# Gate rows of a fused transformer layer moved from the FFN loop to the output projection, and operand-making in wider operations

## The chip, the cores and the metric

The kernel runs on one core of a Trainium2 chip. The metric is device microseconds (us) of one execution. The kernel before took 2268.96 us, the median of three runs between 2266.91 and 2269.43.

Each engine runs its own queue in order: TensorE (PE, with its weight loads as PEld) multiplies, VectorE (DVE) and ScalarE (ACT) work on elements, SyncE (SP) issues the transfers, GpSimd (POOL) does next to nothing here. They wait for each other through semaphores.

## The reference

One layer on x of 512 positions x 2048 features, with a conditioning vector c:

```python
mod = cond @ w_ada[layer] + b_ada[layer]          # cond = silu(c); 6 x 2048 values
sh1, sc1, g1, sh2, sc2, g2 = split(mod, 6)
h = rms_norm(x, norm1_g) * (1 + sc1) + sh1
proj = h @ w_in                                   # 2048 -> 4*1024 + 3*1024
o_hg = hgrn2_mixer(...)                           # 8 heads, gated recurrence
o_sb = stick_breaking_mixer(...)                  # 8 heads, causal attention
x = x + g1 * (concat(o_hg, o_sb) @ w_out)
h = rms_norm(x, norm2_g) * (1 + sc2) + sh2
gate, up = split(h @ w_ffn_in, 2)                 # 2048 -> 2 * 5632
x = x + g2 * ((silu(gate) * up) @ w_ffn_out)
```

What matters here is `mod`: six groups of 2048 values, each a dot product of c with a column of `w_ada`. G1 is needed for the first residual, SC2 and SH2 for the second norm, and G2 only at the very end.

## The kernel before

All matrix products are of fp32 accuracy: each operand is split in a high and a low part (`S.copy` to fp32r on ACT, then `V.tensor_sub` on DVE), and three matmuls (hi x hi, hi x lo, lo x hi) stand for one. A weight split is line 231 (ACT) and line 232 (DVE); `three` and `product` issue the matmuls, all recorded under line 93.

A **row** of `mod` is one call of `ada(comp, k)` (line 186): 128 of the values, from a 1 MiB load into a buffer of the "raw" ring (four buffers, shared with all weight loads; line 175) and a multiply-and-sum on DVE over 128x2048 elements (line 179, called a gemv here). There are 16 rows to each of the six groups, 96 in all. `rest` is the list of those not yet done.

The program goes through these stages, with times of the profiled execution:

1. Norm, first projections and stick-breaking heads, up to about 440 us.
2. **Gated stage**, 440 to 770 us: eight HGRN2 heads. `hg_project` gives PE long runs of projection matmuls with 512 columns; `hg_attend` is a chain of "levels" (five small steps of DVE, ACT and PE that wait for each other), put between the projection matmuls. Where each step goes is fixed as the program is built: `Clock` adds up a modelled time of the matmuls, and a side task that yields a number from the table `Y` continues when the clock has passed it. `tasks_every(Y["hgtask"], rest[:HG_TASKS])` is such a side task: one row every 30 units, 8 of them (SC2 rows 8 to 15).
3. **Output projection**, 770 to 952 us: 16 column tiles m, each of 16 k-blocks (48 matmuls of 512 columns, about 10.9 us). A tile loads its weight (`wo8r` is tile 8's), splits it in two halves a tile ahead, and ends with the residual on DVE (line 874), a store of x1 to DRAM, a square on ACT and a sum on DVE. The loop over m then takes rows from `rest`: before, two behind m = 0 and 1 and one behind m = 2 to 13, the 16 SH2 rows.
4. **Second norm and first two FFN tiles**, 946 to 1001 us. The last column tile is done in two halves of 256 positions. `normed` multiplies a 128x256 block by the norm (DVE) and applies gain and shift (ACT, line 899); `make_first` and `make_second` split the blocks into the operands that `first_part` multiplies by `wff`. The results are held until DVE has formed the operands for products 6, 7, 5 and 4 (opB, opC).
5. **FFN loop**, 1001 to 1827.6 us: matrices f = 2 to 43. Each loads 2 x 1 MiB (`wg`, `wu`), forms sums of weight blocks, splits seven of them, and multiplies in seven products of 24 matmuls with 256 columns, in the order 1, 2, 6, 7, 5, 4, 3 (Strassen's scheme). Products 1, 6, 5, 3 add up in one accumulator, ffA, and ACT copies its value out between them (`tap`, line 1030: a, b, u); ffB has product 2, ffC 7 and 4 (tap c). `keep` multiplies the activations of a pair of matrices, and `one_later` spreads what follows of it (names `forms`, `fhi`) over the next matrix. Behind each matrix one row of `rest` is taken: before, the 16 G2 rows behind f = 2 to 17.
6. FFN output, 1827 to 2266 us.

Within a stage a scheduler sets the order of each engine's queue by priority and by the program's order; the ring's buffers set when a load can be issued.

Of the kernel before, what the change touches and what calls it, by code (L numbers as in the profile page):

```python
# [24 lines left out]
HT = 256  # L25
HALF = 8
# [1 line left out]
ORDER = (2, 1, 7, 6, 4, 5, 3)  # L28
AHEAD = 300
SC2_EARLY = 8  # L30
HG_TASKS = 8
EARLY = 3
Y = {"norm": 7.0, "qk": 5.0, "z": 4.0, "aA": 10.0, "oA": 2.0, "aB": 4.5, "oB": 2.5,
     "base": 6.5, "level": 2.2, "r1": 3.0, "r2": 2.4, "ho": 1.8,
     "settle": 20.0, "shrow": 6.0, "fix": 2.6, "hgtask": 30.0, "task": 5.0}
EPS = 1e-6
TINY = 1e-30
LN_TINY_CAP = 44.0
# [7 lines left out]
SH1, SC1, G1, SH2, SC2, G2 = range(6)  # L46
# [35 lines left out]
def view(t, off, dims):  # L82
    return bass.AP(tensor=t.tensor, offset=t.offset + off, ap=[list(t.ap[0])] + [list(d) for d in dims])
# [46 lines left out]
def trunk(ctx, tc, a):  # L130
    nc = tc.nc
    V, S, G = nc.vector, nc.scalar, nc.gpsimd
# [31 lines left out]
    gain2 = const.tile([P, KT], F32, name="gain2")  # L164
# [132 lines left out]
    for k in range(KT):  # L297
        xk = xo[:, k]
        if k == 0:
# [3 lines left out]
            j = SC1 * KT  # L303
# [196 lines left out]
    rb = sb.tile([P, T], F32, tag="I", name="rb1", bufs=1)  # L500
# [28 lines left out]
    shrow = xo[:, 0:4].rearrange("p a b -> p (a b)")  # L529
# [256 lines left out]
    hgx = ExitStack()  # L786
    hg = hgx.enter_context(tc.tile_pool(name="hg", bufs=1))
    clock.start(hg_heads())
    rest = [partial(ada, SC2, k) for k in range(SC2_EARLY, KT)] + [partial(ada, SH2, k) for k in range(KT)]
    clock.start(tasks_every(Y["hgtask"], rest[:HG_TASKS]))  # L790
    for h in range(NH):
        if h:
# [49 lines left out]
    x1 = xop.tile([P, KT, T], F32, tag="xo", name="x1")  # L842
# [23 lines left out]
    for m in range(KT - 1):  # L866
        xr = load_x(m)
        if m < 2:
            wo_part(m, 0, [last])
        else:  # L870
            if m > 3:
                wo_part(m, 8, head)
            wo_part(m, 0, tail)
        V.scalar_tensor_tensor(x1[:, m], wo[m], mcol(G1, m), xr, op0=ALU.mult, op1=ALU.add)
        nc.sync.dma_start(x1d[:, m], x1[:, m])
        add_square(m)
        for _ in range(2 if m < 14 and len(rest) > 14 - m else 1):
            if rest:
                rest.pop(0)()

# [8 lines left out]
    def block(kh, th, j):
        return x1[:, kh * HALF + j, th * HT:th * HT + HT]  # L890

    def split_to(p, j, src):
        S.copy(H[p][:, j, 0], src)
        V.tensor_sub(H[p][:, j, 1], src, H[p][:, j, 0].bitcast(F32))

    def normed(kh, th, j):
        k, hs = kh * HALF + j, slice(th * HT, th * HT + HT)
        V.tensor_mul(x1[:, k, hs], x1[:, k, hs], rb[:, hs])
        S.activation(x1[:, k, hs], x1[:, k, hs], AF.Identity, scale=gain2[:, k:k + 1], bias=mcol(SH2, k))

    def make_first(j):
        for kh in range(2):
            normed(kh, 0, j)
            split_to(1 + kh, j, block(kh, 0, j))
            parts[kh, 0, j] = H[1 + kh][:, j, 0], H[1 + kh][:, j, 1]

    def make_second(j):
        normed(0, 1, j)
        t = ft.tile([P, 2, HT], F32R, tag="t", name=f"b12_{j}")
        S.copy(t[:, 0], block(0, 1, j))  # L910
        V.tensor_sub(t[:, 1], block(0, 1, j), t[:, 0].bitcast(F32))
        parts[0, 1, j] = t[:, 0], t[:, 1]
        normed(1, 1, j)
        split_to(3, j, block(1, 1, j))
        parts[1, 1, j] = H[3][:, j, 0], H[3][:, j, 1]
# [10 lines left out]
    m = KT - 1  # L926
# [4 lines left out]
    rb = ft.tile([P, T], F32, tag="ss2", name="rb2", bufs=2)  # L931
    for i, hs in enumerate(halves):
        out = acc(f"wo{m}h{i}")[:, 0:HT]
        n = 0
        for c0, (whi, wlo) in ((8, w8), (0, w0)):
            for kk in range(8):
                three(out, whi[:, kk], wlo[:, kk], ohi[:, c0 + kk, hs], olo[:, c0 + kk, hs], n == 0, n == KT - 1)
                n += 1
        V.scalar_tensor_tensor(x1[:, m, hs], out, mcol(G1, m), xr[:, hs], op0=ALU.mult, op1=ALU.add)
        nc.sync.dma_start(x1d[:, m, hs], x1[:, m, hs])  # L940
        sq = ft.tile([P, HT], F32, tag="t", name=f"sql{i}")
        S.activation(sq, x1[:, m, hs], AF.Square)
        ps = att(f"ssum2{i}")[:, 0:HT]
        PE.matmul(ps, ones, ss2[:, hs], start=True, stop=False)
        PE.matmul(ps, ones, sq, start=False, stop=True)
        av = ft.tile([P, HT], F32, tag="t", name=f"av2{i}")
        tmp = ft.tile([P, HT], F32, tag="t", name=f"tmp2{i}")
        y = rb[:, hs]
        S.activation(y, ps, AF.Ln, bias=epsb, scale=1.0 / D)
        V.tensor_scalar(av, ps, 1.0 / D, EPS, op0=ALU.mult, op1=ALU.add)  # L950
        S.activation(y, y, AF.Exp, scale=-0.5)
        newton(y, av, tmp)
        if i == 0:
            for k in range(EARLY):
                make_first(k)

    for j in range(HALF):
        if j >= EARLY:
            make_first(j)
        make_second(j)  # L960


    first = [[acc(f"ff{j}")[:, 0:HT] for j in range(4)], [att(f"ff{j + 4}")[:, 0:HT] for j in range(2)]]
# [32 lines left out]
    for j in range(HALF):
        V.tensor_sub(block(0, 0, j), block(0, 1, j), block(0, 0, j))
        t2 = ft.tile([P, HT], F32, tag="t", name=f"t2_{j}")
        V.tensor_sub(t2, block(1, 1, j), block(0, 0, j))
        split_to(6, j, t2)  # L1000
        V.tensor_sub(block(1, 0, j), block(1, 0, j), t2)
    for j in range(HALF):
        V.tensor_sub(block(0, 1, j), block(1, 1, j), block(0, 1, j))
        split_to(7, j, block(0, 1, j))
    for j in range(HALF):
        split_to(5, j, block(0, 0, j))
    for j in range(HALF):
        split_to(4, j, block(1, 0, j))
# [47 lines left out]
    def begin_second():  # L1056
# [11 lines left out]
        for q in range(4, 7):  # L1068
            load_op(0, q)
        yraw.append(fg.tile([P, 2, 4, T], F32, tag="b22", name="yraw"))  # L1070

    rest += [partial(ada, G2, k) for k in range(KT)]

    forms = {}

# [53 lines left out]
    for f in range(2, FM):  # L1131
        A11, A12 = halves_of(load(a["w_fi"][f, 0], [P, KT, P], f"wg{f}"))
        A21, A22 = halves_of(load(a["w_fi"][f, 1], [P, KT, P], f"wu{f}"))
        S1 = tp.tile([P, HALF, P], F32, tag="sum", name=f"ffS{f}", bufs=3)
        A, B, C = acc(f"ffA{f}")[:, 0:HT], acc(f"ffB{f}")[:, 0:HT], att(f"ffC{f}")[:, 0:HT]
        w1, w2 = operand(A11, f"ff{f}_1"), operand(A12, f"ff{f}_2")
        with tc.high_priority(offset=AHEAD):
            V.tensor_add(S1, A21, A22)
# [12 lines left out]
        t_c = tap(C, f"c{f}")
        one_later()
        product(A, operand(S1, f"ff{f}_5"), 5)
        tu = tap(A, f"u{f}")
        one_later()
        product(C, operand(A22, f"ff{f}_4"), 4)
        one_later()
        product(A, operand(A12, f"ff{f}_3", False), 3)

        sg = tp.tile([P, T], F32, tag="sg", name=f"sg{f}", bufs=2)  # L1160
        up = tp.tile([P, T], F32, tag="up", name=f"up{f}", bufs=1)
        with tc.high_priority(offset=2 * AHEAD if f == FM - 1 else 0):
            V.tensor_add(sg[:, 0:HT], B, ta)
            S.activation(sg[:, 0:HT], sg[:, 0:HT], AF.Silu)
# [82 lines left out]
    for u, (c, i) in enumerate(units):  # L1247
# [16 lines left out]
        t2 = (T2[0] if u else yraw[0][:, 2])[:, 0:CHUNKS[c]]  # L1264
# [113 lines left out]
```

## Time and profile before

| | |
|---|---|
| median of three runs | 2268.96 us |
| profiled execution | 2268.31 us |
| its span in the trace | 2266.5 us |
| mean granted TensorE clock | 0.994 |
| DMA, mean over the span | 193 GB/s, 437.68 MB |
| rows of `mod` by line 179 | 95, 217 us of DVE (mean 2286 ns) |
| DVE waiting for a row's load | 36 us |

The span runs from the first to the last instruction that the profiler recorded; the execution's own time is 1.8 us longer. Busy times are shares of the span. A wait is told as "engine, line it waits at <- engine and line that released it: total, times, longest". In a timeline row stand the start, the duration, the engine, the line, and what is read and written; brackets at its end give the wait just before it and what ended it. A window row gives busy time (and number of instructions) of each engine in a stretch, the granted clock of PE, the DMA engines' busy share and their rate. SPq is the queue of transfers that SP issues.

### The profile page before, as it was taken

Reading aid. Unit: us, or ns where it says so; the run is one execution under the profiler, and the core shown is the slowest. Engines: PE = TensorE matmul, PEld = TensorE weight load, DVE = VectorE, ACT = ScalarE, POOL = GpSimd, SP = SyncE. Lnnn points to the kernel's source line nnn. Section 1 sums busy time; section 2 is a strip of 40 time slices with the busy share of each in tenths; the row PEclk is TensorE's granted clock in tenths of the full one; section 3 lists DMA queues with packets and bytes.
Section 4 is the critical chain, followed back from the end, with each engine's and each line's share of the span. In section 5 each row is a group of like instructions: output and inputs, shape, how many; then the busy total and the mean of one; then the engine's idle time right before and its main releaser. Section 6 shows DMA issues by size and latency. Waiting matters only on the chain. (4 is left out here: it accounts for less than half of the span.)

```text
span 2266.5 us, 35532 instructions
## 1 busy us (share of the span) xinstructions
PE 2221.9 (98%) x14171; PEld 2025.4 (89%) x14171; DVE 1912.1 (84%) x2566; ACT 1157.3 (51%) x2015; POOL 10.1 (0%) x25
## 2 busy tenths in 40 slices
PE   7999899999999999999999999999999999999999
PEld 6899899978888888899999999999999987788887
DVE  8886778899888875599899988888888888898888
ACT  4315666566565622475444545555455554545453
POOL 0000000000000000000000000000000000000000
PEclk9999999999999999999999999999999999999999
DMA  9885546763232296326565554535454486666452
GB/s 371 314 319 215 178 142 232 288 228 112 93 112 75 83 327 250 111 103 228 205 215 201 195 181 145 176 131 177 142 172 150 159 333 248 241 223 223 163 198 67
DMA packets 115265, 437.68 MB, mean 193 GB/s; under 512 B 9854, under 2 KB 58268, under 8 KB 77340
## 3 DMA queue, kind: packets, MB, share of 16 engines
q1 hardware_dynamic: 115100, 435.42, 53.7%
q8 instruction: 111, 1.82, 0.3%
q14 instruction: 54, 0.44, 0.1%
HBM read 386.61 MB, written 48.77 MB: 192 GB/s over the span
## 5 line engine op out<-in xcount | busy, mean ns | idle before, releaser
L93 PE MATMUL sbp<-wsb,hhi 128*128 128x384 f32 x1024 | 271.2, 344 | 3.1 <-DVE wsb L232 1.7
L179 DVE SCALAR_TENSOR_TENSOR ada<-ada,cond 128x2048 f32<-128x2048 f32 x95 | 216.7, 2286 | 36.3 <-DMA ada<-in_w_ada 36.1
L93 PEld LDWEIGHTS sbp<-wsb,hhi 128*128 128x128 f32 x1024 | 186.3, 191 | 8.0 <-issue 3.3
L93 PE MATMUL sbp<-wsb,hlo 128*128 128x384 f32 x512 | 173.6, 339 | 0.0
L93 PE MATMUL wo<-ohi,wo 128*128 128x512 f32 x480 | 149.5, 391 | 2.0 <-ACT ohi L808 2.0
L232 DVE TENSOR_TENSOR wfo<-wfo,wfo 128x1024 fp32r<-128x1024 f32 (+1 forms) x72 | 83.5, 1163 | 31.7 <-ACT wfo L231 31.5
L93 PEld LDWEIGHTS wo<-ohi,wo 128*128 128x128 f32 x480 | 89.8, 188 | 21.0 <-ACT ohi L808 2.6
L231 ACT CAST wfo<-wfo 128x1024 fp32r<-128x1024 f32 (+1 forms) x72 | 72.5, 1007 | 63.2 <-PE foA L93 53.8
L93 PEld LDWEIGHTS sbp<-wsb,hlo 128*128 128x128 f32 x512 | 97.6, 191 | 0.8 <-issue 0.5
L93 PE MATMUL ffA<-opD,ff 128*128 128x256 f32 x768 | 97.3, 283 | 0.0
L93 PE MATMUL ffA<-opB,ff 128*128 128x256 f32 x768 | 93.3, 277 | 1.6 <-ACT ff L231 1.2
L93 PEld LDWEIGHTS ffA<-opD,ff 128*128 128x128 f32 x768 | 94.2, 191 | 0.0
L93 PE MATMUL ffC<-opC,ff 128*128 128x256 f32 x768 | 93.7, 278 | 0.4 <-ACT c L1030 0.4
L93 PE MATMUL wo<-olo,wo 128*128 128x512 f32 x240 | 93.3, 390 | 0.0
L93 PE MATMUL ffA<-opC,ff 128*128 128x256 f32 x744 | 90.3, 277 | 2.3 <-ACT b L1030 2.3
L93 PE MATMUL ffB<-opA,ff 128*128 128x256 f32 x768 | 92.4, 276 | 0.0
L93 PEld LDWEIGHTS ffA<-opB,ff 128*128 128x128 f32 x768 | 90.2, 189 | 2.0 <-ACT ff L231 1.4
L93 PEld LDWEIGHTS ffC<-opC,ff 128*128 128x128 f32 x768 | 90.3, 188 | 1.1 <-ACT c L1030 1.0
L93 PE MATMUL ffA<-opA,ff 128*128 128x256 f32 x744 | 89.7, 276 | 0.8 <-DVE ff L232 0.8
L93 PEld LDWEIGHTS ffA<-opC,ff 128*128 128x128 f32 x744 | 87.0, 188 | 3.2 <-ACT b L1030 3.1
L93 PEld LDWEIGHTS ffB<-opA,ff 128*128 128x128 f32 x768 | 89.5, 188 | 0.0
L93 PE MATMUL ffC<-opB,ff 128*128 128x256 f32 x744 | 89.5, 276 | 0.0
(1004 smaller groups left out, 5906.2 us busy)
## 6 DMA issues: line engine op xcount, KB each, us to landing
ada<-in_w_ada SPq DMA_DIRECT2D x95, 1024.0 KB, 6.0
wfo<-in_w_fo SPq DMA_DIRECT2D x16, 1024.0 KB, 5.0
yraw<-in_w_fo SPq DMA_DIRECT2D x16, 1024.0 KB, 5.0
fix<-in_w_fix SPq DMA_DIRECT2D x14, 1024.0 KB, 6.1
opd<-forms SPq DMA_DIRECT2D x44, 256.0 KB, 3.5
opd<-fhi SPq DMA_DIRECT2D x42, 256.0 KB, 4.2
opsC<-opd SPq DMA_DIRECT2D x10, 1024.0 KB, 6.6
opsA<-opd SPq DMA_DIRECT2D x9, 1024.0 KB, 5.7
```

The costliest lines, as they stand in the source:

```text
L93: self.engine.matmul(out, lhsT, rhs, **kw)
L179: V.scalar_tensor_tensor(w, w, 1.0, row, op0=ALU.mult, op1=ALU.mult, accum_out=col)
L231: S.copy(hi, r)
L232: last_lo[0] = V.tensor_sub(lo, r, hi.bitcast(F32)).ins
```

## The change

Rows of `mod`: 14 instead of 8 in the gated stage (SC2 8 to 15, then SH2 0 to 5), one every 21.5 units instead of 30. The output projection takes the other 26 (SH2 6 to 15 and all of G2), one behind each of the tiles 0 to 3 and two behind 4 to 14. None is left for the FFN loop. The number of rows is the same.

```diff
-HG_TASKS = 8
+HG_TASKS = 14
-     "settle": 20.0, "shrow": 6.0, "fix": 2.6, "hgtask": 30.0, "task": 5.0}
+     "settle": 20.0, "shrow": 6.0, "fix": 2.6, "hgtask": 21.5, "task": 5.0}
-    rest = [partial(ada, SC2, k) for k in range(SC2_EARLY, KT)] + [partial(ada, SH2, k) for k in range(KT)]
+    rest = [partial(ada, SC2, k) for k in range(SC2_EARLY, KT)]
+    rest += [partial(ada, comp, k) for comp in (SH2, G2) for k in range(KT)]
...
-        for _ in range(2 if m < 14 and len(rest) > 14 - m else 1):
+        for _ in range(1 if m < 4 else 2):
             if rest:
                 rest.pop(0)()
...
-    rest += [partial(ada, G2, k) for k in range(KT)]
...
-        if rest:
-            rest.pop(0)()
```

Wider operations: `normed` multiplies the two feature halves (kh = 0 and 1) of one or two blocks j in one DVE operation; `make_first` splits as many in one cast and one subtraction; `make_second` works on pairs of j but for its low half b12, which stays at one; the operands opB and opC are made for pairs of j. The order of blocks is changed with it: the first block of `make_second` comes ahead, then pairs alternate.

```diff
-    def normed(kh, th, j):
-        k, hs = kh * HALF + j, slice(th * HT, th * HT + HT)
-        V.tensor_mul(x1[:, k, hs], x1[:, k, hs], rb[:, hs])
-        S.activation(x1[:, k, hs], x1[:, k, hs], AF.Identity, scale=gain2[:, k:k + 1], bias=mcol(SH2, k))
+    def both(th, j, n):
+        return view(x1, j * T + th * HT, [[HALF * T, 2], [T, n], [1, HT]])
+    def normed(th, j, n):
+        V.tensor_mul(both(th, j, n), both(th, j, n), view(rb, th * HT, [[0, 2], [0, n], [1, HT]]))
+        for jj in range(j, j + n):
+            for kh in range(2):
+                k = kh * HALF + jj
+                b = block(kh, th, jj)[:, 0]
+                S.activation(b, b, AF.Identity, scale=gain2[:, k:k + 1], bias=mcol(SH2, k))
+    def make_first(j, n):
+        normed(0, j, n)
+        hi, lo = (early[:, :, j:j + n, i] for i in range(2))
+        S.copy(hi, both(0, j, n))
+        V.tensor_sub(lo, both(0, j, n), hi.bitcast(F32))
...
+    make_second(0, 1)
+    for j in range(1, HALF):
+        if j == EARLY:
+            make_first(j, 1)
+        elif j > EARLY and j % 2 == 0:
+            make_first(j, 2)
+        if j % 2:
+            make_second(j, min(2, HALF - j))
...
-    for j in range(HALF):
-        V.tensor_sub(block(0, 1, j), block(1, 1, j), block(0, 1, j))
-        split_to(7, j, block(0, 1, j))
+    for j in range(0, HALF, 2):
+        V.tensor_sub(block(0, 1, j, 2), block(1, 1, j, 2), block(0, 1, j, 2))
+        split_to(7, j, 2, block(0, 1, j, 2))
```

What stands where on the engines, at three places. Names end in numbers that count tiles; they differ between the two kernels for the same tile.

DVE in the FFN loop around the operands of f = 7, before: `ff7_1`, `ff7_2`, `ff7_6` are the splits for products 1, 2 and 6, `wg7r` and `ffS7` the weight and its sum, `forms` and `fhi5` belong to the pair of f = 4 and 5, and `ada85` is a gate row.

```order
L1106 TENSOR_TENSOR forms4_9353<-forms4_9353,fhi5_0_9686 128x768
L232 TENSOR_TENSOR ff7_1lo2_9830<-wg7r_9821,ff7_1hi2_9829 128x1024
L179 SCALAR_TENSOR_TENSOR ada85_10045,mod_79<-ada85_10045,cond_72 128x2048
L232 TENSOR_TENSOR ff7_2_9833<-wg7r_9821,ff7_2_9833 128x1024
L1140 TENSOR_TENSOR wg7r_9821<-ffS7_9825,wg7r_9821 128x1024
L1106 TENSOR_TENSOR forms4_9353<-forms4_9353,fhi5_3_9750 128x512
L1141 TENSOR_TENSOR wg7r_9821<-wg7r_9821 128x1024
L232 TENSOR_TENSOR ff7_6_9895<-wg7r_9821,ff7_6_9895 128x1024
```

The same place of the changed kernel:

```order
L1118 TENSOR_TENSOR forms4_9297<-forms4_9297,fhi5_0_9624 128x768
L232 TENSOR_TENSOR ff7_1lo2_9765<-wg7r_9756,ff7_1hi2_9764 128x1024
L1152 TENSOR_TENSOR wg7r_9756<-ffS7_9760,wg7r_9756 128x1024
L1177 TENSOR_TENSOR up6_9748<-u6_9686,c6_9657 128x256
L232 TENSOR_TENSOR ff7_2_9768<-wg7r_9756,ff7_2_9768 128x1024
L1118 TENSOR_TENSOR forms4_9297<-forms4_9297,fhi5_3_9688 128x512
L1153 TENSOR_TENSOR wg7r_9756<-wg7r_9756 128x1024
L232 TENSOR_TENSOR ff7_6_9830<-wg7r_9756,ff7_6_9830 128x1024
```

The gate row between the splits of products 1 and 2 is gone; the sum for product 6 (line 1140, now 1152) and the sum of f = 6 that `keep` waits for (line 1177) stand ahead of the split of product 2.

SP's transfers in the output projection from tile 8's weight to tile 10's, before: `wo` are weights, `ada` rows, `x1d` the store of a residual, `xr` the load of x for the next one.

```order
L206 DMA wo8r_7352<-in_w_out 128x2048
L175 DMA ada58_7413<-in_w_ada 128x2048
L875 DMA x1d_6971<-x1_6961 128x512
L863 DMA xr6_7215<-in_x 128x512
L206 DMA wo9r_7419<-in_w_out 128x2048
L175 DMA ada59_7480<-in_w_ada 128x2048
L206 DMA wo10r_7486<-in_w_out 128x2048
```

From the same weight to the same weight in the changed kernel:

```order
L206 DMA wo8r_7377<-in_w_out 128x2048
L175 DMA ada82_7438<-in_w_ada 128x2048
L876 DMA x1d_6989<-x1_6979 128x512
L864 DMA xr7_7304<-in_x 128x512
L175 DMA ada83_7441<-in_w_ada 128x2048
L206 DMA wo9r_7447<-in_w_out 128x2048
L175 DMA ada84_7508<-in_w_ada 128x2048
L876 DMA x1d_6989<-x1_6979 128x512
L864 DMA xr8_7374<-in_x 128x512
L175 DMA ada85_7511<-in_w_ada 128x2048
L206 DMA wo10r_7517<-in_w_out 128x2048
```

A tile now issues two rows, the second of them behind the store and the load of x.

DVE in the gated stage at a late level of head 6, before: `QB6`, `KB6` are the scaled operands of a level, `dgs6` a masked diagonal block, `whq7` a projection weight of head 7 and `hgg6`, `scr` the gate of head 6.

```order
L709 TENSOR_TENSOR KB6_3_6294<-KEY_6_5904,ES6_3_6290 128x2x16x8
L232 TENSOR_TENSOR whq7_0_6419<-whq7r_6417,whq7_0_6419 128x1024
L673 COPY_PREDICATED dgs6_6172<-msk_90,l6_2_6284 128x512
L708 TENSOR_TENSOR QB6_4_6316<-Q_6_5905,EP6_4_6312 128x2x8x16
L622 SCALAR_TENSOR_TENSOR scr_92<-hgg6_6162,scr_92 128x512
L709 TENSOR_TENSOR KB6_4_6317<-KEY_6_5904,ES6_4_6313 128x2x8x16
```

The same place of the changed kernel:

```order
L709 TENSOR_TENSOR KB6_3_6303<-KEY_6_5915,ES6_3_6299 128x2x16x8
L179 SCALAR_TENSOR_TENSOR ada53_6755,mod_79<-ada53_6755,cond_72 128x2048
L232 TENSOR_TENSOR whq7_0_6431<-whq7r_6429,whq7_0_6431 128x1024
L622 SCALAR_TENSOR_TENSOR scr_92<-hgg6_6171,scr_92 128x512
L673 COPY_PREDICATED dgs6_6181<-msk_90,l6_2_6293 128x512
L708 TENSOR_TENSOR QB6_4_6328<-Q_6_5916,EP6_4_6324 128x2x8x16
L624 TENSOR_TENSOR SG_6_6170<-hgg6_6171,scr_92 128x512
L709 TENSOR_TENSOR KB6_4_6329<-KEY_6_5915,ES6_4_6325 128x2x8x16
```

A row now stands inside this head's chain of levels, and two steps of its gate (lines 622 and 624) stand earlier between them.

More of the change, by code (lines that the diff above doesn't have):

```diff
@@ L887, in trunk @@
     parts = {}
[L889 to L894, printed above, removed]
-    def normed(kh, th, j):
-        k, hs = kh * HALF + j, slice(th * HT, th * HT + HT)
-        V.tensor_mul(x1[:, k, hs], x1[:, k, hs], rb[:, hs])
[L899 to L915, printed above, removed]
+    def block(kh, th, j, n=1):
+        return x1[:, kh * HALF + j:kh * HALF + j + n, th * HT:th * HT + HT]
+    def both(th, j, n):
+        return view(x1, j * T + th * HT, [[HALF * T, 2], [T, n], [1, HT]])
@@ new lines, in split_to @@
+    def split_to(p, j, n, src):
+        hi, lo = (H[p][:, j:j + n, i] for i in range(2))
+        S.copy(hi, src)
+        V.tensor_sub(lo, src, hi.bitcast(F32))
+    def normed(th, j, n):
[5 more added lines that the diff above has]
+                S.activation(b, b, AF.Identity, scale=gain2[:, k:k + 1], bias=mcol(SH2, k))
@@ new lines, in make_first, with make_second @@
+    def make_first(j, n):
[3 more added lines that the diff above has]
+        V.tensor_sub(lo, both(0, j, n), hi.bitcast(F32))
+        for jj in range(j, j + n):
+            for kh in range(2):
+                parts[kh, 0, jj] = H[1 + kh][:, jj, 0], H[1 + kh][:, jj, 1]
+    def make_second(j, n):
+        normed(1, j, n)
+        for jj in range(j, j + n):
+            t = ft.tile([P, 2, HT], F32R, tag="t", name=f"b12_{jj}")
+            src = block(0, 1, jj)[:, 0]
+            S.copy(t[:, 0], src)
+            V.tensor_sub(t[:, 1], src, t[:, 0].bitcast(F32))
+            parts[0, 1, jj] = t[:, 0], t[:, 1]
+            parts[1, 1, jj] = H[3][:, jj, 0], H[3][:, jj, 1]
+        split_to(3, j, n, block(1, 1, j, n))
@@ L954, in trunk @@
             for k in range(EARLY):
-                make_first(k)
-    for j in range(HALF):
-        if j >= EARLY:
-            make_first(j)
-        make_second(j)
+                make_first(k, 1)
+    make_second(0, 1)
[6 more added lines that the diff above has]
+            make_second(j, min(2, HALF - j))
     first = [[acc(f"ff{j}")[:, 0:HT] for j in range(4)], [att(f"ff{j + 4}")[:, 0:HT] for j in range(2)]]
@@ L995, in trunk @@
     H.update({6: late[:, 0], 7: late[:, 1], 5: later[:, 0], 4: later[:, 1]})
[L996 to L1002, printed above, removed]
-        V.tensor_sub(block(0, 1, j), block(1, 1, j), block(0, 1, j))
-        split_to(7, j, block(0, 1, j))
[L1005 to L1008, printed above, removed]
+    for j in range(0, HALF, 2):
+        V.tensor_sub(block(0, 0, j, 2), block(0, 1, j, 2), block(0, 0, j, 2))
+        t2 = ft.tile([P, 2, HT], F32, tag="t", name=f"t2_{j}")
+        V.tensor_sub(t2, block(1, 1, j, 2), block(0, 0, j, 2))
+        split_to(6, j, 2, t2)
+        V.tensor_sub(block(1, 0, j, 2), block(1, 0, j, 2), t2)
+    for j in range(0, HALF, 2):
+        V.tensor_sub(block(0, 1, j, 2), block(1, 1, j, 2), block(0, 1, j, 2))
+        split_to(7, j, 2, block(0, 1, j, 2))
+    for j in range(0, HALF, 2):
+        split_to(5, j, 2, block(0, 0, j, 2))
+    for j in range(0, HALF, 2):
+        split_to(4, j, 2, block(1, 0, j, 2))
     fctx.close()
```

## The prediction

> **What bounds the kernel now.** I read the page first, then the busy time of each engine by stages, then TensorE's waits, then the timeline at the places those named.
>
> ```profile
> span 2266.5 us, 35532 instructions
> PE 2221.9 (98%) x14171; PEld 2025.4 (89%) x14171; DVE 1912.1 (84%) x2566; ACT 1157.3 (51%) x2015; POOL 10.1 (0%) x25
> ```
>
> TensorE (PE) is busy for 98% of the span, and no matmul is removed, so only time in which PE waits or runs slowly can be won. The windows give one row for each stretch: gated stage, output projection, the FFN loop in two pieces, and two single matrices of it, f = 2 and f = 7.
>
> ```profile
> core 0: us, PE busy (x) PEld busy (x) DVE busy (x) ACT busy (x) POOL busy (x), PEclk, DMA share, GB/s
> 460.00:760.00 300.00, 298.94 (x1532) 250.84 (x1531) 259.85 (x502) 181.83 (x404) 8.38 (x16) 1.00 0.31 113
> 815.00:946.00 131.00, 131.00 (x602) 109.47 (x601) 71.11 (x75) 33.40 (x39) 0.00 (x0) 1.00 0.66 231
> 1001.00:1320.00 319.00, 310.21 (x2648) 307.68 (x2647) 295.44 (x337) 154.69 (x233) 0.00 (x0) 0.99 0.58 202
> 1320.00:1820.00 500.00, 498.21 (x4348) 497.70 (x4347) 423.43 (x481) 258.58 (x378) 0.00 (x0) 1.00 0.46 160
> 1001.00:1026.90 25.90, 22.23 (x171) 21.43 (x169) 25.90 (x33) 11.12 (x17) 0.00 (x0) 0.93 0.42 140
> 1103.70:1128.19 24.49, 21.53 (x170) 21.13 (x169) 20.71 (x26) 9.11 (x14) 0.00 (x0) 0.93 0.65 227
> ```
>
> PE idles 8.8 us in 1001 to 1320, against 1.8 us in the longer piece behind it. VectorE (DVE) is 93% busy in the first and 85% in the second. The rows of one gemv operation name the difference, and PE's waits in 1000 to 1345 show where it ends.
>
> ```profile
> L179 DVE SCALAR_TENSOR_TENSOR ada<-ada,cond x16: 2278/2291/2294, 1017.2 to 1302.0; 128x2048 f32<-128x2048 f32 x16
> L179 DVE DVE_READ_ACCUMULATOR ada<-ada,cond x16: 80/82/85, 1019.4 to 1304.2; 128x1 f32 x16
> PE ffA L93 <- ACT b L1030: 5.2, 5, 2.6
> PE ffC L93 <- ACT ff_7hi L231: 1.6, 1, 1.6
> PE ffA L93 <- ACT ff L231: 1.2, 1, 1.2
> PE ffA L93 <- DVE ff L232: 0.8, 1, 0.8
> ```
>
> Those waits understate the loss, since a late matmul partly hides in its modelled end. The pace of the loop shows it whole: first matmul of matrix f = 2, 7, 19 and 20 on PE's timeline, and the loop's end on the chain that ended last.
>
> ```profile
> 1001.01 0.39 PE L93 MATMUL ffA<-opA,ff 128*128 128x256 f32 x2
> ...
> 1103.70 0.39 PE L93 MATMUL ffA<-opA,ff_1hi 128*128 128x256 f32 x2
> ...
> 1346.07 0.39 PE L93 MATMUL ffA<-opA,ff_1hi 128*128 128x256 f32 x2
> 1365.27 0.50 PE L93 MATMUL ffA<-opA,ff 128*128 128x256 f32 x3
> 1827.60 4.11 PE foB L93 x18
> ```
>
> An undisturbed matrix takes 1365.27 - 1346.07 = 19.20 us. The first 17 (f = 2 to 18) take 345.06 instead of 17 x 19.20 = 326.40: **18.66 us are lost** where a gemv row is in the loop, 25.89 - 19.20 = 6.69 of it in f = 2 and 24.49 - 19.20 = 5.29 in f = 7, the two single windows above. The 25 behind take 481.53 instead of 480.00: 1.53 lost.
>
> How a gemv row does that is seen in f = 7, in order of time over four engines:
>
> ```profile
> 1101.45 2.28 DVE L179 SCALAR_TENSOR_TENSOR ada<-ada,cond 128x2048 f32<-128x2048 f32 x1
> 1103.77 0.34 SPq L206 DMA_DIRECT2D wu8r<-in_w_fi  x1
> 1112.98 1.23 DVE L1138 TENSOR_TENSOR ffS<-wu8r 128x1024 f32<-128x1024 f32 x1 [2.29 <-DMA wu8r<-in_w_fi]
> 1117.44 0.42 ACT L1164 ACTIVATE sg<-sg 128x256 f32<-128x256 f32 x1 [6.37 <-DVE sg L1163]
> 1118.17 0.79 PE L93 MATMUL ffA<-opC,ff_5hi 128*128 128x256 f32 x2 [2.60 <-ACT b L1030]
> ```
>
> The load of wu8 needs a buffer of the "raw" ring, is issued as the gemv ends, lands late, DVE stands still for it, ScalarE (ACT) waits for DVE, and the copy of product A queued behind on ACT is what PE waits for. So the row costs 2.37 us on DVE and a place in the ring of four.
>
> **The change, part by part.** The sum starts from the profiled execution, 2268.31 us (span 2266.5 and 1.8 around it); the median of the runs shown lies 0.65 above.
>
> *The 16 gate rows leave the loop.* Removed: 16 x (2.29 + 0.08) = 38 us of DVE, 16 loads and 16 ring places. That takes DVE from 295 to about 257 of 319 us, 81%, below the piece that already runs free. I let f = 3 to 18 lose what that piece loses, 1.53 / 25 x 16 = 1.0. Matrix f = 2 has other causes too: DVE runs without a pause through its 25.9 us, with splits still to be made. The wider operations help there. Two rows give the widths:
>
> ```profile
> 773.97 4.89 DVE L809 TENSOR_TENSOR olo<-xo,ohi 128x512 fp32r<-128x512 f32 x8
> 998.26 2.77 DVE L894 TENSOR_TENSOR opC<-x,opC 128x256 fp32r<-128x256 f32 x8
> ```
>
> A 256-wide one costs 0.34 us and a 512-wide one 0.60, so a merged pair saves 0.07. The late operands merge 64 into 32 (2.2 us); the first ones 56 (32 of the norm, 16 + 8 splits) into 22, some of them four blocks wide (about 2.3). DVE thus reaches f = 2 some 4.5 us sooner, but its second operation there needs the held products, which end with the first tiles' last matmuls. Walking its order from there at 1.14 us for each 1024-wide operation, the cast for product 7 comes about 0.45 us and that for product 6 about 1.1 us late, against waits of 0.8 + 1.6 + 1.2 before. I take 2.0 us for f = 2 (0.8 to 6.7). Gain in the loop: 18.66 - 1.0 - 2.0 = **15.7 us** (8 to 18.7).
>
> Part of this is clock. The two slow matrices show PEclk 0.93, so each ran about 0.07 x 25 = 1.8 us short of cycles. [...]
>
> *Six more rows in the gated stage, every 21.5 instead of 30 units.* The windows of line 179 alone give what stands there now:
>
> ```profile
> 470.00:769.00 299.00, 21.12 (x20) 1.00 0.30 106
> ```
>
> Twenty records are ten rows, since each has a second one that reads the sum. Six more add 14 us of DVE to 260 of 300, 91%. In the same 299 us the list of PE's waits is empty, with some of the ten inside a head's chain of levels. The added ones put 2.37 us into more such chains (head 6 is printed above); the static order answers by moving the later level matmuls of heads 2, 3, 5 and 6 back by 5 to 11 projection matmuls of 0.23 us, 1.1 to 2.5 us. What is left over, up to 1.2 us, may wait four times. I take +1.0 (0 to 5); nothing excludes the lower end, since PE's queue there is full of projection matmuls.
>
> *22 rows, two per tile, in the output projection.* DVE's work per tile becomes two splits, two gemvs, one residual and one sum, 2 x 1.14 + 2 x 2.37 + 0.75 + 0.69 = 8.5 us, in a tile of 10.88. What counts is the loop through SP's queue: the second row's load stands behind the store of the residual x1 and the next x load; DVE does the gemv before the next residual. One round of before, with the two halves of the next split:
>
> ```profile
> 874.97 0.75 DVE L874 SCALAR_TENSOR_TENSOR x<-wo,mod,xr 128x512 f32<-128x512 f32 x1 [0.45 <-PE wo L93]
> 876.64 0.44 SPq L175 DMA_DIRECT2D ada<-in_w_ada  x1
> 883.44 2.29 DVE L179 SCALAR_TENSOR_TENSOR ada<-ada,cond 128x2048 f32<-128x2048 f32 x1 [0.67 <-DMA ada<-in_w_ada]
> 885.85 0.75 DVE L874 SCALAR_TENSOR_TENSOR x<-wo,mod,xr 128x512 f32<-128x512 f32 x1
> 886.98 1.23 DVE L232 TENSOR_TENSOR wo<-wo11r,wo 128x1024 fp32r<-128x1024 f32 x1 [0.38 <-ACT wo L231]
> 893.40 1.22 DVE L232 TENSOR_TENSOR wo<-wo11r,wo 128x1024 fp32r<-128x1024 f32 x1
> 896.73 0.75 DVE L874 SCALAR_TENSOR_TENSOR x<-wo,mod,xr 128x512 f32<-128x512 f32 x1 [2.02 <-PE wo L93]
> ```
>
> The load takes 6.80 us from issue to gemv, and residual to residual is 10.88, so the loop just closes. Where loads are denser it takes longer:
>
> ```profile
> 833.11 0.42 SPq L175 DMA_DIRECT2D ada<-in_w_ada  x1
> 841.23 2.29 DVE L179 SCALAR_TENSOR_TENSOR ada<-ada,cond 128x2048 f32<-128x2048 f32 x1 [2.03 <-DMA ada<-in_w_ada]
> ```
>
> With 8.12 us, DVE would fall back 1.2 to 1.3 us per tile, 11 to 12 over nine double tiles. Tile 11's matmuls start with the end of tile 10 at 896.7, and its first half-split is done at 888.2; the second is done at 894.6 and needed half a tile later, at 902.1. So 7.5 us of lag cost PE nothing; the tiles behind, without gemvs, let DVE catch up. Cost: 0 (0 to 4.5); the cover is the split made one tile ahead, and beyond it each us of lag is a us of PE. I take 0, by the row whose neighbours are most like the new order (one store, one x load, one weight).
>
> *Wider normalising.* At the start of the first FFN tiles PE waits for ACT's cast b:
>
> ```profile
> 963.12 2.05 PE L93 MATMUL ff<-b,wff 128*128 128x256 f32 x12 [0.43 <-ACT b L910]
> 961.69 1.09 ACT L899 ACTIVATE x<-x,mod,gain 128x256 f32<-128x256 f32 x2
> ```
>
> ACT now does two more normalisations of later blocks before it, 0.5 us each, and five wide casts instead of ten narrow ones: some 0.5 to 1.3 us later. I take +0.8 (-0.5 to +2).
>
> Sum: 2268.3 - 15.7 + 1.0 + 0 + 0.8 = 2254.4, and with the median's 0.65, **2255**.
>
> **The rivals.**
> 1. *The loop frees itself only partly.* Weight loads still arrive late without gemvs (DVE's longest wait behind 1346 is below), and f = 2 may wait for the same held products, with the clock drop. If f = 2 keeps its 6.7 and the others a third of their 12, the gain is 8: 2268.3 - 8 + 1.8 = 2262. For it: f = 2 has no slack before the held products, and this row of the gemv-free piece:
>
> ```profile
> DVE ffS L1138 <- DMA wu34r<-in_w_fi: 3.0, 1, 3.0
> ```
>     Against: such late loads cost PE only 1.53 us in 25 matrices.
> 2. *The gated stage gives it back.* If each of the six added rows holds up a level chain by its full 2.37 us, 14.2 replaces the 1.0: 2267.6, no change. Against: no PE wait there with ten rows.
> 3. *Slower: the loads of the projection.* A tile must move 3 MiB of weights and 0.5 MiB of x1 and x, 3.67 MB in 10.88 us, 337 GB/s, where the stage now has 231. If a gemv's load takes L, the lag is 9 x (L - 6.9) and PE pays what exceeds 7.5. The gain of 13.9 is used up at L = 9.3 us; at 10.5 the stage pays 24.9 and the time is 2279. For it: wu8's load took up to 9.2 us (1103.77 to 1112.98). Against: a longer tile also thins the traffic.
>
> **How the numbers follow.** Forecast (2249 to 2259) 0.58; partly freed (to 2264.5) 0.22; cancelled 0.13; slower 0.07. The range 2249 to 2264.5 leaves out 0.2; its lower end is the whole 18.7 won with no cost. A measurement of this kernel tells 0.2% (4.5 us) from no change, so faster is 0.80, the same 0.13, slower 0.07.
>
> **What would show it.** Right: no L179 row behind 960; f = 2 under 22 us and f = 3 to 18 at 19.20; clock 1.00 from 1000 to 1320; no PE wait on a wo split; DVE near 79% between 831 and 929. Wrong: f = 2 still at 25 us (rival 1), PE waits at level matmuls between 470 and 769 (rival 2), residuals later and later behind their matmuls and PE waiting for wo (rival 3).

## The result and the profile after

The changed kernel takes 2251.15 us, the median of four runs (2250.58 to 2252.8), against 2267.99 before (four runs, 2266.91 to 2269.43). The ratio is 0.9928, with a 95% interval of 0.9914 to 0.9941: faster by 17 us, inside the predicted range and 3.9 us below the forecast of 2255.

The page of the changed kernel, first the span and then busy time of each engine:

```profile
span 2248.8 us, 35433 instructions
PE 2214.3 (98%) x14171; PEld 2018.7 (90%) x14171; DVE 1914.2 (85%) x2500; ACT 1160.4 (52%) x1986; POOL 10.1 (0%) x25
```

PE is busy 7.6 us less with the same 14171 matmuls: part of the time won had stood in the trace as slow matmuls and not as waits. The windows of the same stretches as before, in the same columns:

```profile
460.00:760.00 300.00, 298.84 (x1528) 249.53 (x1527) 270.58 (x513) 181.61 (x402) 8.37 (x16) 1.00 0.37 133
815.00:946.00 131.00, 131.00 (x605) 109.50 (x604) 92.58 (x94) 31.64 (x37) 0.00 (x0) 1.00 0.85 313
1001.00:1320.00 319.00, 317.56 (x2766) 316.82 (x2766) 276.16 (x314) 166.21 (x243) 0.00 (x0) 1.00 0.45 156
1320.00:1820.00 500.00, 500.00 (x4334) 498.30 (x4333) 423.89 (x480) 259.61 (x379) 0.00 (x0) 1.00 0.48 170
1000.48:1022.32 21.84, 20.40 (x170) 19.81 (x169) 21.58 (x23) 11.88 (x17) 0.00 (x0) 1.00 0.43 158
```

The output projection (815 to 946) carries 313 GB/s instead of 231 and 21.5 us more of DVE, and PE does not stop in it. In the loop's first piece PE's busy time rises from 310.2 to 317.6 of 319, the granted clock from 0.99 to 1.00, and the traffic falls from 202 to 156 GB/s. The last of these window rows is matrix f = 2. PE's waits in 1000 to 1345 have shrunk to two, both in f = 2:

```profile
PE ffA L93 <- ACT ff L231: 1.0, 1, 1.0
PE ffC L93 <- ACT ff_7hi L231: 0.5, 1, 0.5
```

The pace of the loop, by the first matmul of f = 2, 3 and 19 on PE's timeline and the loop's end on the chain that ended last:

```profile
1000.48 0.39 PE L93 MATMUL ffA<-opA,ff 128*128 128x256 f32 x2
...
1022.32 0.28 PE L93 MATMUL ffA<-opA,ff_1hi 128*128 128x256 f32 x1
...
1330.09 0.28 PE L93 MATMUL ffA<-opA,ff_1hi 128*128 128x256 f32 x1
...
1810.26 4.11 PE foB L93 x18
```

f = 2 takes 21.84 us instead of 25.89, f = 2 to 18 take 329.61 instead of 345.06, and the 25 matrices behind 480.17 instead of 481.53. An undisturbed 17 would take 326.40, so 3.21 us are still lost, against 18.66 before. (The chain's row starts 0.17 us behind the first matmul of the stage that follows the loop; from there, as in the table below, the 25 matrices take 480.00, against 481.37 before.)

Where the 17.7 us between the two profiled executions (2268.31 and 2250.58) came from, by the first matmul of each stage in the two traces:

| stretch | before | after | difference |
|---|---|---|---|
| start to the first `hgq` matmul, a projection of the gated heads | 453.65 | 451.93 | -1.7 |
| gated stage, from there to the first matmul of the output projection | 316.26 | 317.30 | +1.0 |
| output projection, tiles 0 to 14 | 170.14 | 169.15 | -1.0 |
| last tile, norm, first two FFN tiles | 60.96 | 62.09 | +1.1 |
| FFN loop | 826.42 | 809.61 | -16.8 |
| rest | 440.9 | 440.5 | -0.4 |

### The profile page after: what moved, and what is told of

Its sections match the earlier page's. It is cut to its first block, busy times and chain, and to the rows that moved or that the text cites. A ratio compares the mean times of both kernels' runs of the same rounds, so it can differ in the third digit from the quotient of the medians.

```text
span 2248.8 us, 35433 instructions
## 1 busy us (share of the span) xinstructions
PE 2214.3 (98%) x14171; PEld 2018.7 (90%) x14171; DVE 1914.2 (85%) x2500; ACT 1160.4 (52%) x1986; POOL 10.1 (0%) x25
## 4 chain that ended last, share of the span: by engine, by line
PE 91%; DVE 6%; issue 2%; ACT 1%; DMA 0%; SPq 0%; DVEq 0%; ACTq 0%
PE ffA L93 21%; PE foA L93 10%; PE ffC L93 10%; PE sbp L93 8%; PE wo L93 7%; PE foC L93 5%; PE ffB L93 5%; PE st L93 4%; PE hgg L93 4%; PE hgq L93 3%; PE hgf L93 3%; PE foB L93 2%; PE ff L93 2%; DVE ada L179 1%; PE l L93 1%
## 5 line engine op out<-in xcount | busy, mean ns | idle before, releaser
L93 PEld LDWEIGHTS wo<-ohi,wo 128*128 128x128 f32 x480 | 89.9, 188 | 19.8 <-ACT ohi L809 1.5
L93 PE MATMUL st<-wi,hhi 128*128 128x512 f32 x256 | 76.3, 398 | 11.0 <-ACT hhi L317 11.0
```

Of the source, the lines that this page charges most:

```text
L93: self.engine.matmul(out, lhsT, rhs, **kw)
```

## The experiments

"Lost in the loop" is the time from the first matmul of f = 2 to that of f = 19 in the profiled execution, less 17 x 19.20 us. Medians are of the runs that the comparison uses, beside the ratio to the kernel before on the same chip.

| run | median | ratio, 95% interval | lost in f = 2 to 18 |
|---|---|---|---|
| before | 2268 to 2269 | 1 | 18.7 |
| changed kernel | 2251.2 | 0.9928 (0.9914 to 0.9941) | 3.2 |
| again | 2252.4 | 0.9933 (0.9919 to 0.9947) | 3.9 |
| rows_only | 2256.3 | 0.9945 (0.9932 to 0.9957) | 7.3 |
| wide_only | 2265.3 | 0.9990 (0.9981 to 0.9999) | 17.3 |
| place_only | 2264.7 | 0.9981 (0.9969 to 0.9993) | 18.3 |
| dve_only | 2254.9 | 0.9941 (0.9928 to 0.9955) | 4.4 |
| traffic_only | 2251.6 | 0.9926 (0.9913 to 0.9940) | 2.9 |
| all_but_place | 2257.9 | 0.9957 (0.9943 to 0.9970) | 9.0 |
| hg10 | 2258.5 | 0.9954 (0.9940 to 0.9967) | 3.2 |
| three_rows | 2275.3 | 1.0025 (1.0016 to 1.0034) | 3.9 |
| late_keep | 2251.3 | 0.9919 (0.9906 to 0.9931) | 2.4 |
| late_hold | 2249.9 | 0.9918 (0.9903 to 0.9933) | 2.0 |

### Which half of the change: rows_only and wide_only

rows_only is the kernel before with `HG_TASKS`, `hgtask`, `rest` and the two loops that take from it as in the change, and no wider operation. wide_only is the other half.

> The rows moved as in the change, every operation as narrow as before. Theory A (the rows in the loop cost the time; wide operations only shorten the second norm's backlog into f = 2): f = 3 to 43 at 19.20 us, f = 2 still near 25, time 2251.2 + 3 to 4 = 2254 to 2255. Rival B (the wide operations do nothing that shows): f = 2 near 21.8 as in the changed kernel, 2251 to 2252. Rival C (the width is what frees VectorE for the loop): losses stay in the loop, 2260 or more.

> The wide operations alone, 8 rows in the gated stage, 16 in the projection and 16 in the loop as before. Theory A: f = 7 and the scattered losses of f = 3 to 18 stay (about 12 us), f = 2 falls from 25.9 to about 23, the first FFN tiles are 0.9 longer: 2265 to 2267. Rival B: 2268. Rival C: 2258 or less.

Windows of f = 2 in rows_only, then of f = 2 and f = 7 in wide_only:

```profile
998.96:1024.85 25.89, 22.41 (x171) 21.61 (x170) 24.92 (x31) 11.14 (x16) 0.00 (x0) 0.93 0.38 133
```

```profile
1000.62:1022.45 21.83, 20.39 (x171) 19.80 (x169) 21.57 (x24) 11.13 (x17) 0.00 (x0) 1.00 0.50 160
1099.41:1124.03 24.62, 21.69 (x171) 21.29 (x170) 20.82 (x24) 9.47 (x15) 0.00 (x0) 0.93 0.66 228
```

With the rows gone and the operations narrow, f = 2 takes 25.89 us as before, to the hundredth, with its clock at 0.93; with wide operations and a row still in it, 21.83. So the 4.05 us won in f = 2 are the wide operations' alone, and the row in f = 2 cost nothing. f = 7 is the reverse: 24.62 in wide_only, 19.20 in rows_only. Theory A held: 2256.3, 1.3 above its number, and 2265.3, inside it. The price of the wide operations is seen too: from the first FFN tile to f = 2 it is 48.16 us in the kernel before and in rows_only, 49.05 in wide_only.

### What of a row costs: its place, its time, its traffic

Four kernels put parts of a row back into f = 2 to 17 of the changed kernel, behind `keep`; the rows themselves are still done in the projection. The output is the same.

```diff
+        if f < 18:                                   # place_only
+            w = row_load(a["w_ada"][G2 * KT + f - 2], f"again{f}")
+            V.tensor_add(dummy, dummy, w[:, 0:1])
...
+        if f < 18:                                   # dve_only
+            V.tensor_add(cond[:, 0:1], cond[:, 0:1], w1[1][:, 0, 0:1].bitcast(F32))
+            V.scalar_tensor_tensor(cond, cond, 0.25, cond, op0=ALU.mult, op1=ALU.mult, accum_out=dummy)
...
+        if f < 18:                                   # traffic_only
+            nc.sync.dma_start(cond, a["w_ada"][G2 * KT + f - 2])
+            V.tensor_add(dummy, cond[:, 0:1], w1[1][:, 0, 0:1].bitcast(F32))
...
+        if f < 18:                                   # all_but_place
+            nc.sync.dma_start(cond, a["w_ada"][G2 * KT + f - 2])
+            V.tensor_add(cond[:, 0:1], cond[:, 0:1], w1[1][:, 0, 0:1].bitcast(F32))
+            V.scalar_tensor_tensor(cond, cond, 0.25, cond, op0=ALU.mult, op1=ALU.mult, accum_out=dummy)
```

`dummy` is a column of `mod` that is no longer needed, `cond` the conditioning vector, read for the last time in the projection; the 128x1 operation on the split of product 1 keeps the long one at its old place in VectorE's order.

> The changed kernel with the 16 loads of gate rows put back into the loop, each read by VectorE in one 128x1 operation where the long one stood: the ring place and the traffic without the 2.37 us. Theory P (the ring place makes weight loads late): at least half of the loop's loss comes back, 2258 to 2265, with waits of VectorE for a wu load. Rival D (VectorE's 2.37 us are what counts): 2251 to 2252.

> The changed kernel with 16 operations of 128x2048 put back into VectorE's order of the loop at the same place, on data that is there already: 2.37 us each and no load, no ring place. Theory P: little, 2251 to 2255, f = 7 at 19.20. Rival D: 2260 to 2266, most of it in f = 2 and f = 7.

> The changed kernel with 16 loads of 1 MiB in the loop again, but into a buffer of their own (that of the conditioning vector, which is free by then) and not the raw ring; VectorE reads each in one 128x1 operation. It differs from place_only by the ring place alone. Theory P (the ring place): 2251 to 2254, VectorE's waits for wu loads as in the changed kernel. Rival T (16 MiB more traffic, or the wait for the row itself, makes the weights late): 2258 to 2265 as place_only.

> The changed kernel with the whole cost of a gate row put back into f = 2 to 17, but for the place in the raw ring: a load of 1 MiB into the conditioning vector's buffer, and the 128x2048 operation on it. Theory P (the place is the main cost; traffic nothing, VectorE's time 2.5 us in the loop): 2254 to 2255.5. Rival S (load and time together make the loop's loss, the place adds nothing): the 824 of wide_only in the loop, 2264 to 2266.

place_only brings the loss back, 18.3 us in the loop and 15.1 more than in the changed kernel, with 0.16 us of VectorE for each row instead of 2.4. By the medians it is 13.5 us, since its profiled execution, 2267.8, is one of the slower. Its matrix f = 9, on four engines in order of time:

```profile
1134.60 0.33 SPq L175 DMA_DIRECT2D again<-in_w_ada  x1
...
1137.36 0.80 SPq L206 DMA_DIRECT2D wg10r<-in_w_fi  x1
...
1139.99 0.51 SPq L206 DMA_DIRECT2D wu10r<-in_w_fi  x1
...
1142.50 0.28 PE L93 MATMUL ffA<-opA,ff 128*128 128x256 f32 x1
...
1149.86 1.23 DVE L1150 TENSOR_TENSOR ffS<-wu10r 128x1024 f32<-128x1024 f32 x1 [3.15 <-DMA wu10r<-in_w_fi]
...
1154.45 0.42 ACT L1176 ACTIVATE sg<-sg 128x256 f32<-128x256 f32 x1 [5.26 <-DVE sg L1175]
...
1155.71 0.36 ACT L1046 COPY b<-ffA 128x256 f32<-128x256 f32 x1
...
1156.13 0.39 PE L93 MATMUL ffA<-opC,ff 128*128 128x256 f32 x1 [2.58 <-ACT b L1046]
```

The two weights' loads and the first matmul of f = 9 in the changed kernel, on SP's and PE's timeline:

```profile
1127.75 0.33 SPq L206 DMA_DIRECT2D wg10r<-in_w_fi  x1
...
1131.16 0.85 SPq L206 DMA_DIRECT2D wu10r<-in_w_fi  x1
...
1138.09 0.28 PE L93 MATMUL ffA<-opA,ff 128*128 128x256 f32 x1
```

What is late is the issue of wu10 more than its load: 2.5 us ahead of the matrix in place_only and 6.9 in the changed kernel, where the load takes 8.8 us from issue to use, against 9.9, and PE doesn't wait. In the changed kernel wg10 is issued as the last split of wu8 ends (1127.7); in place_only the end of the same split (1134.6) lets the row's load go, and the two weights follow 2.8 and 5.4 us behind.

From there it is the chain that the prediction read in f = 7 of the kernel before, link by link: late weight, VectorE standing, `sg` on ScalarE, the copy b behind it, PE. No long operation is needed for it. traffic_only differs from place_only in the buffer that the load goes to (and in the tie of its 128x1 operation to that split), and loses nothing: 2251.6, with 205 GB/s in 1001 to 1320, as much as the kernel before had:

```profile
1001.00:1320.00 319.00, 317.57 (x2769) 316.97 (x2768) 278.31 (x330) 166.59 (x243) 0.00 (x0) 1.00 0.58 205
```

One thing goes away together with the place: VectorE's waits for the rows' own loads, 14.7 us in ten waits in place_only and none in traffic_only. What of the loss is by late weights and what by VectorE standing for a late row isn't separated; in f = 9 it is the weight.

dve_only has VectorE at 306.4 of those 319 us, more than the kernel before, and loses 1.2 us more than the changed kernel in f = 2 to 18 (3.7 us more by the medians). So theory P stands against D and T. all_but_place came out between P (2254 to 2255.5) and S (2264 to 2266): 2257.9. 4.7 us of its excess are in one matrix, f = 4:

```profile
1043.73:1067.59 23.86, 21.73 (x171) 21.12 (x169) 23.06 (x30) 10.40 (x15) 0.00 (x0) 0.93 0.65 230
```

VectorE is busy for 23.06 of its 23.86 us, with one of the long operations in it and one just ahead, PE waits three times for 0.7 us, and the granted clock was 0.93. Just why the backlog came there wasn't tried. The parts are thus not additive: in the profiled executions, load and time without the place cost 5.8 us of the loop, the place with its load 15.1, all three together (wide_only) 14.1. The place is enough for the loss, and some 8 us of it need it. place_only spreads from 2256.7 to 2270.6, where nine runs of the changed kernel lie between 2250.6 and 2255.8; what varies so from run to run, one trace can't show.

### How far the projection and the gated stage go: hg10 and three_rows

```diff
-HG_TASKS = 14                                        # hg10
+HG_TASKS = 10
-        for _ in range(1 if m < 4 else 2):
+        for _ in range(2):
...
-        for _ in range(1 if m < 4 else 2):           # three_rows
+        for _ in range(1 if m < 4 else 3):
```

hg10 also sets `hgtask` to 30.

> The changed kernel with 10 rows in the gated stage, every 30 units, and two rows behind each of the 15 projection tiles. If the six added rows made the gated stage 1.0 longer (316.3 to 317.3), four of them fewer give back 0.7: 2250.5, stage 316.6. Rival: the projection's first tiles pay for the second row, 2252 to 2255, with PE waits on wo splits between 770 and 815.

> The changed kernel with three rows behind tiles 4 to 10 and one behind 11. A tile then moves 4 MiB of weights and 0.5 MiB of x and x1, 4.72 MB; at the 354 GB/s of the first 100 us that is 13.3 us instead of 10.88. Theory of the projection's limit (loads): lag 7 x 2.4 = 17, less the cover of 7.5: PE waits 10, 2261. Rival (only VectorE counts, 3 x 2.37 + 3.7 = 10.8 us a tile): 2251 to 2252.

hg10's gated stage takes 316.63 us, 0.67 less than the changed kernel's 317.30 for four rows fewer, as expected; but its tiles 0 to 14 take 173.74 instead of 169.15, and the rival was right about the projection, though not about the place: PE waits for tiles 5 and 6, at 831 to 845 us, and not between 770 and 815. The median, 2258.5, is beyond the rival's numbers too; the profiled execution, 2254.6, is the fastest of five, so 4 us of the median stand in no trace. The weights of tiles 5 and 6 are issued late, behind pairs of rows, and PE waits for tile 6's cast, which waited for its load. SP's, ScalarE's and PE's timeline in hg10:

```profile
834.22 0.49 SPq L206 DMA_DIRECT2D wo6r<-in_w_out  x1
...
842.50 1.99 ACT L231 CAST wo<-wo6r 128x1024 fp32r<-128x1024 f32 x2 [8.44 <-DMA wo6r<-in_w_out]
...
843.60 0.50 PE L93 MATMUL wo<-ohi,wo 128*128 128x512 f32 x1 [1.28 <-ACT wo L231]
```

three_rows took 191.89 us for the same tiles, 22.7 more, where the limit by the loads' rate gave 10. The direction was right and the size was not. VectorE's, SP's and ScalarE's timeline around tile 8 of three_rows shows how a tile runs there:

```profile
854.42 2.36 DVE L232 TENSOR_TENSOR wo<-wo7r,wo 128x1024 fp32r<-128x1024 f32 x2 [0.65 <-ACT wo L231]
...
856.81 0.33 SPq L206 DMA_DIRECT2D wo8r<-in_w_out  x1
...
868.06 0.75 DVE L875 SCALAR_TENSOR_TENSOR x<-wo,mod,xr 128x512 f32<-128x512 f32 x1 [3.00 <-PE wo L93]
...
868.90 0.63 ACT L859 ACTIVATE sq<-x 128x512 f32<-128x512 f32 x1 [13.04 <-DVE x L875]
869.44 1.98 ACT L231 CAST wo<-wo8r 128x1024 fp32r<-128x1024 f32 x2
...
870.50 2.36 DVE L232 TENSOR_TENSOR wo<-wo8r,wo 128x1024 fp32r<-128x1024 f32 x2 [0.24 <-ACT wo L231]
```

Three rows and one weight fill the ring of four. The next weight is issued only when the last one is split (856.78, then 856.81), so none is loaded a tile ahead, and its cast is no longer made during the tile ahead either: on ScalarE it stands behind the square of that tile's residual. The load itself, by the view of transfers,

```profile
wo8r<-in_w_out SPq DMA_DIRECT2D x1, 1024.0 KB, 8.3
```

lands 8.3 us behind its issue, at 865.1, and 4.3 us ahead of the cast. What the cast waits for is the square, the square the residual, and the residual the tile's last matmul. So matmuls, residual, square, cast and split follow one behind the other: 870.50 - 854.42 = 16.1 us, and 15.4 for the tile behind. That the order of ScalarE's queue follows from the late load is likely and was not tried. It is not the loads' rate: these tiles move less than the double tiles of the changed kernel. Windows of three_rows, then of the changed kernel:

```profile
890.00:920.00 30.00, 24.07 (x97) 18.52 (x97) 20.81 (x21) 5.03 (x6) 0.00 (x0) 0.96 0.81 310
```

```profile
831.00:929.00 98.00, 98.00 (x434) 81.16 (x433) 74.73 (x74) 23.52 (x27) 0.00 (x0) 1.00 0.89 332
```

Part of the 22.7 is clock: PE stands for 11.5 us in five waits for a cast, the longest 2.5, and the granted clock was 0.96 in 815 to 968 and 0.90 in 860 to 890, where the changed kernel had 1.00 in 815 to 946; 0.04 x 153, some 6 us, is an estimate of what that cost.

### What f = 2 still loses: late_keep, late_hold, again

```diff
-    for f in range(2):                               # late_keep
-        keep(f, held[:, 2 * f], held[:, 2 * f + 1])
...
+            diff = V.tensor_sub(A21, A11, A21).ins
...
+        if f == 2:
+            with tc.issue_after(diff):
+                for g in range(2):
+                    keep(g, held[:, 2 * g], held[:, 2 * g + 1])
```

late_hold moves `hold(1)` with them, ahead of the `for g` line.

> The changed kernel with the products of the held gates and ups put behind the first sums of f = 2 in VectorE's order. Theory H (f = 2 loses its 2.6 us since VectorE stands 1.5 us for the held copies, with the sums behind): f = 2 at 19.2 to 20, f = 3 at 19.2 to 19.8, 2248.5 to 2249.5. Rival: the held buffer is a ring place, wu3 comes later and f = 3 or 4 gives it back, 2251 or more.

> The changed kernel once more, beside the next two on the same chip: 2251 to 2252, f = 2 at 21.84.

> As late_keep, with ScalarE's copies of the held gates also behind its casts for products 1 and 2 of f = 2 (there VectorE stood 2.5 us for the cast of product 2, queued behind them). If that queue is what f = 2 still loses: f = 2 at 19.2 to 20.0, loop 807 to 807.5, 2 us less than the changed kernel. Rival: the held products come later still and f = 3 or the accumulators wait: no gain.

late_keep changed nothing that can be told (2251.3, f = 2 at 21.63): theory H had the wrong queue. VectorE now stands for ScalarE's cast, which is queued behind the copies of the held gates. VectorE's row in late_keep, and the same operation of late_hold (there two merged):

```profile
1001.89 1.23 DVE L232 TENSOR_TENSOR ff<-wg2r,ff 128x1024 fp32r<-128x1024 f32 x1 [2.47 <-ACT ff L231]
```

```profile
999.53 2.52 DVE L232 TENSOR_TENSOR ff<-wg2r,ff 128x1024 fp32r<-128x1024 f32 x2
```

With the copies behind the casts that wait is gone, f = 2 takes 19.8 us, and the loop 808.4 against 810.3 of "again" on the same chip. The medians are 2249.9 and 2252.4, five runs each; 2.6 us is 0.11%, less than such runs can tell apart, so late_hold is the better by its trace alone.

## Why the prediction was right, step by step

- **The rows leave the loop: 15.7, measured 16.8.** The two terms were f = 2 at 2.0 us of loss (2.64 measured) and f = 3 to 18 at 1.0 (0.57). The rest of the difference is the piece behind f = 18, which I left at its 1.5 of loss and which ran free; wide_only and place_only, with rows or their places in the loop, ran free there too, at 480.00, so the rows are not what made it in the profiled execution of before. The walk through VectorE's order for f = 2 gave the cast for product 7 as 0.45 us late and that for product 6 as 1.1; PE waited 0.5 and 1.0.
- **Its argument by VectorE's share did not hold.** It put VectorE at 257 of 319 us, 81%, below the 85% of the piece that ran free, and took that piece's loss from there. The measured share is 276 of 319, 87%, in part because the faster loop brings 118 more matmuls into the window; and dve_only, at 306 of 319, loses only 1.2 us more. So the share of VectorE does not decide the loss, and that 1.0 came so near 0.57 is in part luck: the 16 ring places that left with the rows, counted in the same sentence and given no price, carried most of it.
- **Its mechanism.** The prediction named two costs of a row, 2.37 us on VectorE and a place in the ring of four, and did not divide the loss. place_only, dve_only and traffic_only do: the place is enough for nearly all of it (13.5 us by the medians, against 14.1 for wide_only), the time costs 1 to 4 us, the traffic nothing that shows. That the row in f = 2 cost nothing, and the wide operations all that was won there, was foreseen only as "other causes too". Rival 1 (f = 2 keeps its 6.7, the others a third of theirs) fell on both counts: 2.64 and 0.57 of 11.97.
- **The gated stage: +1.0, measured +1.04** (316.26 to 317.30). Nine other profiles with 14 rows give 317.2 to 318.2, wide_only with 8 gives 316.37, hg10 with 10 gives 316.63. Rival 2 needed 14.2 and fell: 34 us of gemv stand in that stage now and the list of PE's waits in it has one entry, of 0.2 us. Where the 1.04 lies is not in that list, so the size was right and its account, level matmuls that wait, is not shown.
- **The output projection: 0, measured -1.0 in the profile.** That 1.0 is not of the change either: wide_only, with the projection's rows as before, takes 169.34. The lag that the prediction worked out begins only in the last double tiles, as the rows under this list show: the residual follows the gemv that waited for its load, 11.58 us behind the one ahead of it, 0.7 of lag against a cover of 7.5. VectorE was busy for 76% of 831 to 929, 79% forecast. Rival 3 did not come, though hg10 and three_rows show it a step away; its price was worked out from how long a load takes, where three_rows lost the split a tile ahead to the ring.
- **Wider normalising: +0.8, measured +1.1** (0.9 in the first FFN tiles, 0.2 ahead of them).
- **What made 3.9 us between forecast and result:** beside these, 1.7 us ahead of 452 us, where the change touches nothing. It goes with the clock. In 137 to 264 us it was granted 0.93 in the kernel before and 0.96 in the changed one (the last rows under this list). From the first stick-breaking projection to the first gated one (`hgf`), nine profiles with 0.96 take 335.9 to 336.1 us, two with 0.95 (place_only and late_hold) 337.5 and 337.8, and two with 0.93 (again and before) 337.9 and 338.2. The profiled execution of the kernel before is of the last kind. A sum built on one profiled execution carries such terms.
- **The clock.** Before, the granted clock was 0.93 in f = 2 and f = 7; both drops went with the waits (1.00 in 1001 to 1320 of the changed kernel), and came back where one wait was left in place (0.93 in f = 2 of rows_only and in f = 7 of wide_only). In f = 7 of the kernel before the drop begins at 1117.89, within the wait of 2.60 us that ends at 1118.17.

VectorE's timeline of the changed kernel in the projection, and below it the window of line 179 alone in the gated stage (30 records are 15 rows, where there were ten):

```profile
905.95 0.75 DVE L875 SCALAR_TENSOR_TENSOR x<-wo,mod,xr 128x512 f32<-128x512 f32 x1
...
915.31 2.29 DVE L179 SCALAR_TENSOR_TENSOR ada<-ada,cond 128x2048 f32<-128x2048 f32 x1 [1.56 <-DMA ada<-in_w_ada]
...
917.53 0.75 DVE L875 SCALAR_TENSOR_TENSOR x<-wo,mod,xr 128x512 f32<-128x512 f32 x1
```

```profile
470.00:769.00 299.00, 34.44 (x30) 1.00 0.35 127
```

PE's windows of 137 to 264 us, of the kernel before and then of the changed one (PE busy, granted clock, DMA share and rate):

```profile
137.00:264.00 127.00, 119.61 (x652) 0.93 0.67 247
```

```profile
137.00:264.00 127.00, 119.53 (x663) 0.96 0.67 247
```

## What to carry to other kernels

In this kernel a small job that shares a ring of load buffers with the main loop was paid in buffers more than in its engine time (13.5 us by the medians for the places of 16 rows with their loads, 3.7 for their time on VectorE): ask whose next load cannot be issued while it holds its place. To see which it is, put back the place, the time and the traffic one at a time, each in the same spot of the queue. Work moved into a stage with slack was free here (tiles 0 to 14 took 169.15 us with two rows behind most, 170.14 before) up to the point where that stage's own prefetch lost its last buffer, and then cost steeply (191.89 with three).

## What was not expected of the hardware

In these traces the granted clock does not follow the length of a gap alone. PE's waits in 1000 to 1345 of place_only, and its window of 1001 to 1320:

```profile
PE ffA L93 <- ACT b L1046: 9.1, 6, 2.6
```

```profile
1001.00:1320.00 319.00, 306.30 (x2636) 303.92 (x2634) 260.43 (x312) 157.58 (x234) 0.00 (x0) 1.00 0.57 202
```

Six waits of this kind, up to 2.6 us (2.58 in the row of f = 9 above), and a granted clock of 1.00; a wait of 2.60 in the kernel before, and the two of 1.6 and 1.2 close together, stand in matrices with 0.93, and so do three of 0.7 within 3 us in f = 4 of all_but_place.

The drops are short stretches at half clock. From 100 to 2200 us the trace of the kernel before has four, from 138.26 for 6.83 us, from 250.90 for 10.24, from 1012.07 for 3.42 and from 1117.89 for 3.41; that of the changed kernel has two, from 139.71 for 3.42 and from 252.35 for 6.83. PE's windows of the kernel before at its wait of 2.60, of the stretch at half clock and the 3.42 us ahead of it (PE busy, granted clock, DMA share and rate):

```profile
1114.47:1117.89 3.42, 1.10 (x10) 1.00 0.00 0
1117.89:1121.30 3.41, 3.13 (x14) 0.50 0.73 221
```

PE is idle for 2.3 us of the first. The ends of matmuls are modelled, so this idle time is rough. Why one wait of 2.6 us came with half clock and another did not is not shown: no run moved a wait by itself.

Also, 16 MiB more of loads in the loop (traffic_only, 205 GB/s instead of 156) cost no time that shows while they had a buffer of their own: 2.9 us were lost in f = 2 to 18, against 3.2 in the changed kernel.
